# Feature-major input blocks that begin 0, 16 or 32 bytes into tiles 32 bytes longer

## The chip, the cores and the metric

The kernel runs on one NeuronCore of a Trainium2 chip. The metric is the device time of one execution in microseconds (us); lower is better.

## The reference

The program is the forward pass of a two-layer decoder trunk over 256 tokens with a width of 2048, all in float32. Every layer is: normalise, mix, add to the residual; normalise, SwiGLU, add to the residual.

- Layer 0 mixes with one input projection of 12,336 columns, whose parts feed an mLSTM head group and a Mamba-2 SSD head group (with a causal convolution); both outputs go through one output projection.
- Layer 1 mixes with causal attention of 16 heads (with 256 tokens a query has only its own block) between a projection to q, k, v and an output projection.
- The SwiGLU has 5632 hidden columns: `(silu(x @ w_gate) * (x @ w_up)) @ w_down`.
- A last normalisation ends the trunk.

Almost all of the arithmetic is in products of a 256-row activation with a large weight matrix.

## The kernel before, in words

**Two-part numbers.** Every large product is made of float32r matmuls. A weight tile `raw` is split on the chip into a high part `wh` (ScalarE, L365 and L439) and the rest `wl` (VectorE, L366 and L441). An activation is split the same way into a high and a low part, and three products, high by high, high by low and low by high, are summed in PSUM (L472 to L474, L411 to L413; in `lin_w` the first and the third are one matmul of 512 columns at L381, and the second is one of 256 columns at L385).

**Feature-major activations.** A `KT` object holds one activation with the 2048 features along the partitions: four blocks of 128 partitions by 4 feature groups by 2 parts by 256 tokens, that is 8192 bytes in each partition. A block is written by `turned` (transposes on TensorE into PSUM, then L225 to L229 split them into the block), and then it is only read. Where a KT lives is its `home`. The inputs of the big projections, `xa` (layer 0), `x1`, `x2` and `x3` (written by `normed_later`), have the home `long`. The other KT objects (`mx`, half of `my`, `ha`, `hb`, `o`) live in pools of the current stage. The first half of `my` calls `long` too, by a function of its own.

**What `long` is.** It takes one of six tiles of 8192 bytes a partition from the pool `res`, which lies near the start of the on-chip memory (SBUF). Besides the four blocks of a KT, `qT` and `kT`, and later the two residual tiles `xr_` (`xres`), live there. The pool `res` also has four `small` tiles of 4096 bytes behind the six.

**Order in memory.** Pools are laid one behind the other: `pad`, `res`, `cst`, `sml`, `pad2`, `tmp`, and then the pools of the stage: MIXER, and after it staging tiles for the weights with JOIN, FFN and ATTN in turn. `pad`, `pad2` and the `gap` entries are tiles that nothing reads or writes. As the pools are laid out before, every block of a KT, every weight tile and every `tmp` tile begins at a multiple of 256 bytes.

**Who reads the blocks.** In `lin_w` (q, k, the convolved columns; in layer 1 q and k) the block is the moving operand, streamed through TensorE, and the weights are loaded as the stationary operand. In `lin_a` (v and o) and in `block` (the z columns, both SwiGLUs' gate and up, v of layer 1) a 128-token piece of the block is loaded as the stationary operand, and the weights are streamed. `block` replaces some pairs of feature groups (plan letter S) by seven products with sums of weights and of activations (`acc_e`, `sums`, `skx`, `skh`).

**Order of the work.** TensorE is fed in program order. Weights come by DMA through the SyncE queue into a ring of tiles; the splits have a raised priority; small pieces of the mixers are put between matmuls by a list of due times (`later`, `tick`). A tile of a later stage that lies on memory of an earlier one waits for that one's last user.

The lines that allocate a block and a `long` tile:

```python
    def long(shape, name, dt=F32):
        return res.tile(shape, dt, tag="res", name=name)
...
                self.blocks[b] = self.home([P, 4, 2, T], f"{self.name}{b}", F32R)
```

Of the kernel before, what the change touches and what calls it, by code (L numbers as in the profile page):

```python
# [9 lines left out]
F32 = mybir.dt.float32  # L10
F32R = mybir.dt.float32r
# [6 lines left out]
P = 128  # L18
T = 256
NT = T // P  # L20
D = 2048
# [19 lines left out]
PLAN_H = {4: "PSPSPPPP", 3: "PSPSPP"}  # L41
PLAN_H_LATE = "PPSPSP"
STAGING = tuple({tag: 1} for tag in "raw1 raw2 wh1 wh2 wl1 raw0 wh0 wl0 wl2".split())
MIXER = ({"raw": 4, "wh": 3, "wl": 3}, {"cb": 1}, {"rows": 3}, {"hm": 2}, {"gap": 192}, {"ba": 4}, {"cols": 2}, {"wide": 2})
JOIN = ({"rawx": 1}, {"gap": 256}, {"blk": 2})
FFN = ({"rawx": 1}, {"skh": 2}, {"blk": 4}, {"gf": 4})
ATTN = ({"blk": 4}, {"qk": 4}, {"v": 2}, {"rope": 1, "mask": 1})
# [18 lines left out]
def hybrid_trunk(ctx: ExitStack, tc: tile.TileContext, a: dict, out: bass.AP):  # L66
# [3 lines left out]
    res = ctx.enter_context(tc.tile_pool(name="res", bufs=6))  # L70
    cst = ctx.enter_context(tc.tile_pool(name="cst", bufs=1))
    sml = ctx.enter_context(tc.tile_pool(name="sml", bufs=2))
    pad2 = ctx.enter_context(tc.tile_pool(name="pad2", bufs=1))
    pad2.tile([P, 40], F32, name="pad2")
    tmp = ctx.enter_context(tc.tile_pool(name="tmp", bufs=9))
    psm = ctx.enter_context(tc.tile_pool(name="psm", bufs=1, space=PSUM))
    drp = ctx.enter_context(tc.tile_pool(name="drp", bufs=1, space=DRAM))
# [20 lines left out]
    def open_stage(name, pools):  # L98

        close_stage()
        for guard, pool, tags in open_pool(name, pools):
            stage["guards"].append(guard)
            stage["pools"].append((pool, tags))
        stage["spare"] = any("rawx" in tags for tags in pools)
# [8 lines left out]
    def held_tile(tag, shape, name, dt=F32):  # L116
        for pool, tags in stage["pools"] + staging:
            if tag in tags:
                return pool.tile(shape, dt, tag=tag, name=name, bufs=tags[tag])
        raise KeyError(tag)  # L120
# [21 lines left out]
    def wide(shape, name, dt=F32):  # L142
        return held_tile("wide", shape, name, dt)

    def long(shape, name, dt=F32):
        return res.tile(shape, dt, tag="res", name=name)

    def t2(shape, name, dt=F32):
        return tmp.tile(shape, dt, tag="tmp", name=name)
# [19 lines left out]

    open_stage("m", MIXER)  # L170

# [19 lines left out]
    rows = t2([P, P], "rows")  # L191
# [64 lines left out]
    class KT:  # L256
# [4 lines left out]

        def block(self, b):
            if self.blocks[b] is None:
                self.blocks[b] = self.home([P, 4, 2, T], f"{self.name}{b}", F32R)
            return self.blocks[b]

        def parts(self, k):
# [276 lines left out]

    w_in = a["l0_w_in"]
    xt0 = KT("xa", KD, long)
    ss0 = cst.tile([P, NT, 4], F32, name="ss0")

# [5 lines left out]
    def input_ready(k, last):  # L554
# [15 lines left out]
        elif c < 4 and c > 1 and k == 4 * c - 2:  # L570
            with tc.high_priority(offset=40):
                input_part(c)

    qT = long([P, MH, T], "qT")
    kT = long([P, MH, T], "kT")
    banks_q = lin_w(w_in, C_Q, xt0, KD, ready=input_ready)
    for c in range(4):
# [107 lines left out]
    cols = held_tile("cols", [P, NT, P], "cols")  # L685
# [28 lines left out]
    hm = [held_tile("hm", [P, MH, MDV + 1], f"hm{t}") for t in range(NT)]  # L714
# [85 lines left out]
    cb, y = [], []  # L800
# [92 lines left out]
    def add_blocks(w, kt, row, nk, plans, finish=None, begin=None, whole=None, pairs=None, ahead=((), ())):  # L893

        for q in range(2):
            c0 = 2 * q * STRIP
            dst = [xr_[t][:, c0 + n_ * STRIP:c0 + (n_ + 1) * STRIP] for t in range(NT) for n_ in range(2)]

            def add_all(what):
                for d, x in zip(dst, what):  # L900
                    nc.vector.tensor_add(d, d, x)

            if begin is not None:
                begin(2 * q)
                begin(2 * q + 1)
            final = q and whole is not None
            F, _ = block(((w, c0), (w, c0 + STRIP)), kt, row, nk, plans[q], add_all, 2 if final else 1, pairs and list(pairs),
                         ahead[q])
            if final:
                for t in range(NT):  # L910
                    with tc.high_priority(offset=1600):
                        for i in (2 * t, 2 * t + 1):
                            for n, cut in enumerate(halved if i == 3 else (slice(0, STRIP),)):
                                nc.vector.tensor_add(dst[i][:, cut], dst[i][:, cut], F[i][:, cut])
                                finish(i - 2 * t + 2, t, n, cut)
                        whole(t)
                continue
            with tc.high_priority(offset=1600):
                add_all(F)
            if finish is not None:  # L920
                for s in (2 * q, 2 * q + 1):
                    finish(s)
# [38 lines left out]
    for q in range(2):  # L961
        F, pre = block(tuple((w_in, C_Z + (2 * q + n) * STRIP) for n in range(2)), xt0, 0, KD, PLAN_X if q else PLAN_LATE,
                       ahead=((5, scale_gated, 0),) if q else ((4, sums_of, xt0, 1),))
        if q == 0:
            for s in range(4):
                need(("y", s))
        for i in range(4):
            with tc.high_priority(offset=1600):
                nc.vector.tensor_add(pre[i], pre[i], F[i])
        for t, n, piece in gate_pieces(q):  # L970
            th = t2([P, STRIP], "thz")
            nc.scalar.activation(th, pre[2 * t + n], AF.Tanh, scale=rh0[:, t:t + 1])
            nc.vector.scalar_tensor_tensor(th, th, 1.0, pre[2 * t + n], op0=OP.add, op1=OP.mult)
            nc.vector.scalar_tensor_tensor(piece, th, rh0[:, t:t + 1], piece, op0=OP.mult, op1=OP.mult)
# [17 lines left out]
    def ffn(xt, r, wg_, wu_, wd, name, finish, begin=None, whole=None):  # L992
# [6 lines left out]
        def hidden(hT, i, s, plan):  # L999
            F, pre = block(((wg_, s * STRIP), (wu_, s * STRIP)), xt, 0, KD, plan)  # L1000
            hs = []
            for t in range(NT):
                g, u = F[2 * t], F[2 * t + 1]
                if pre is not None:
                    for p, f in zip(pre[2 * t:2 * t + 2], (g, u)):
                        with tc.high_priority(offset=1600):
                            nc.vector.tensor_add(p, p, f)
                    g, u = pre[2 * t:2 * t + 2]
                h = t2([P, STRIP], "h")
                nc.scalar.activation(h, g, AF.Tanh, scale=rh[:, t:t + 1])  # L1010
                nc.vector.scalar_tensor_tensor(h, h, 1.0, g, op0=OP.add, op1=OP.mult)
                nc.vector.scalar_tensor_tensor(h, u, rr[:, t:t + 1], h, op0=OP.mult, op1=OP.mult)
                hs.append(h)
            transpose_later(hT, i, hs, None, 1, 0)
# [182 lines left out]
```

## Time and profile before

| what | value |
|---|---|
| time, median of two runs | 2580.15 us (2579.81 and 2580.49) |
| the profiled execution: span from the first to the last instruction | 2578.2 us |
| its mean granted TensorE clock | 0.999 |
| TensorE matmuls, busy | 2563.5 us, 99% of the span, 12,222 |
| TensorE weight loads, busy (beside the matmuls) | 2130.7 us, 83% |
| VectorE | 2196.5 us, 85% |
| ScalarE | 1454.3 us, 56% |
| read from HBM | 492.26 MB, 192 GB/s over the span |

The profile shows one execution. "Busy" of TensorE counts a matmul from its start to a modelled end, and consecutive matmuls overlap, so the distance from one start to the next says more than the duration. The profile names instructions by source line, engine, operation, written and read tile; PE is TensorE, PEld its weight loads, DVE VectorE, ACT ScalarE, POOL GpSimd, SP SyncE. The launch adds to the span what lies before the first instruction and after the last: 2580.15 - 2578.2 = 1.95 us against the median.

### The profile page before, as it was taken

What the parts mean: (1) busy time and instruction counts of PE and PEld (TensorE: products, weight loads), DVE (VectorE), ACT (ScalarE), POOL (GpSimd) and SP (SyncE); (2) the same over time, 40 slices, a digit from 0 to 9 for tenths busy, and PEclk for the clock granted to TensorE, in tenths of its full rate; (3) what the DMA queues carried; (4) which work ended last, traced back from release to release, by engine and by line L of the source; (5) the groups of instructions that cost most, each with busy time, mean ns of one, the idle gap of its engine ahead of it and who ended that gap; (6) DMA issues with size and microseconds to landing.
All of it is one profiled execution on the core that took longest, in us unless ns stands there. A gap on an engine that the chain in (4) does not pass through costs nothing.

```text
span 2578.2 us, 32660 instructions
## 1 busy us (share of the span) xinstructions
PE 2563.5 (99%) x12222; PEld 2130.7 (83%) x12222; DVE 2196.5 (85%) x2831; ACT 1454.3 (56%) x1929; POOL 43.6 (2%) x77
## 2 busy tenths in 40 slices
PE   9999999999999999999999999999999999999998
PEld 8888888888888888888888888888888888888887
DVE  6676777799989998899889986767999888988898
ACT  6465665566665554555455665666655545554554
POOL 2000010000000000000000000000000000000000
PEclk9999999999999999999999999999999999999999
DMA  7566576566564656465656556554555655565554
GB/s 237 170 211 182 166 235 182 163 205 212 185 213 163 215 194 212 163 226 188 206 167 225 186 174 229 164 180 146 180 192 200 212 181 199 193 213 191 199 188 154
DMA packets 254767, 496.55 MB, mean 193 GB/s; under 512 B 15704, under 2 KB 16608, under 8 KB 254352
## 3 DMA queue, kind: packets, MB, share of 16 engines
q1 hardware_dynamic: 250384, 483.26, 57.1%
q0 software_dynamic: 2896, 8.51, 1.1%
q10 hardware_dynamic: 1328, 2.70, 0.3%
q8 instruction: 96, 1.57, 0.2%
q14 instruction: 63, 0.52, 0.1%
HBM read 492.26 MB, written 2.14 MB: 192 GB/s over the span
## 4 chain that ended last, share of the span: by engine, by line
PE 90%; DVE 5%; issue 2%; DMA 2%; ACT 1%; SPq 0%; POOL 0%; POOLq 0%; DVEq 0%; ACTq 0%
PE acc_f L473 18%; PE acc_f L474 18%; PE acc_f L472 17%; PE acc_w L381 11%; PE acc_w L385 5%; PE acc_e L472 4%; PE acc_e L473 4%; PE acc_e L474 4%; PE acc_a L412 2%; PE acc_a L413 2%; PE acc_a L411 2%; DVE wl L441 2%; PE p_tr L282 2%; PE p_y L866 1%; DMA raw<-in_l_w_o 1%
## 5 line engine op out<-in xcount | busy, mean ns | idle before, releaser
L439 ACT CAST wh<-raw 128x1024 fp32r<-128x1024 f32 (+1 forms) x577 | 630.0, 1134 | 412.9 <-PE acc_f L474 338.1
L441 DVE TENSOR_TENSOR wl<-raw,wh 128x1024 fp32r<-128x1024 f32 (+1 forms) x577 | 748.7, 1323 | 79.1 <-ACT wh L439 73.8
L474 PE MATMUL acc_f<-wh,x 128*128 128x512 f32 x1122 | 438.2, 391 | 0.0
L473 PE MATMUL acc_f<-wl,x 128*128 128x512 f32 x1122 | 437.5, 390 | 0.1
L472 PE MATMUL acc_f<-wh,x 128*128 128x512 f32 x1122 | 436.5, 391 | 0.0
L366 DVE TENSOR_TENSOR wl<-raw,wh 128x1024 fp32r<-128x1024 f32 (+1 forms) x225 | 271.3, 1218 | 139.8 <-ACT wh L365 137.3
L439 ACT CAST wh<-sums 128x1024 fp32r<-128x1024 f32 x222 | 227.9, 1051 | 225.9 <-PE acc_f L474 137.7
L365 ACT CAST wh<-raw 128x1024 fp32r<-128x1024 f32 (+1 forms) x225 | 231.9, 1044 | 196.3 <-PE acc_w L381 111.6
L441 DVE TENSOR_TENSOR wl<-sums,wh 128x1024 fp32r<-128x1024 f32 x222 | 266.7, 1221 | 34.6 <-ACT wh L439 34.1
L473 PEld LDWEIGHTS acc_f<-wl,x 128*128 128x128 f32 x1122 | 210.7, 188 | 44.9 <-DVE wl L441 1.9
L474 PEld LDWEIGHTS acc_f<-wh,x 128*128 128x128 f32 x1122 | 210.7, 188 | 43.1
L472 PEld LDWEIGHTS acc_f<-wh,x 128*128 128x128 f32 x1122 | 210.6, 188 | 42.6
L381 PE MATMUL acc_w<-xa,wh 128*128 128x512 f32 x768 | 207.5, 398 | 1.5 <-DVE xa L229 1.5
L381 PEld LDWEIGHTS acc_w<-xa,wh 128*128 128x128 f32 x768 | 138.8, 189 | 27.9 <-DVE xa L229 1.6
L448 DVE TENSOR_TENSOR sums<-raw 128x1024 f32<-128x1024 f32 x111 | 135.4, 1220 | 12.9 <-DMA raw<-in_l_ffn_up 8.0
L381 PE MATMUL acc_w<-x,wh 128*128 128x512 f32 x512 | 138.9, 399 | 0.0
L385 PE MATMUL acc_w<-xa,wl 128*128 128x256 f32 x768 | 121.8, 282 | 0.0
L385 PEld LDWEIGHTS acc_w<-xa,wl 128*128 128x128 f32 x768 | 110.1, 190 | 6.7
L474 PE MATMUL acc_f<-wh,hb 128*128 128x512 f32 (+1 forms) x284 | 109.6, 387 | 0.0
L473 PE MATMUL acc_f<-wl,hb 128*128 128x512 f32 (+1 forms) x284 | 109.6, 387 | 0.0
L472 PE MATMUL acc_f<-wh,hb 128*128 128x512 f32 (+1 forms) x284 | 109.5, 387 | 0.0
L472 PE MATMUL acc_f<-wh,ha 128*128 128x512 f32 x280 | 109.0, 390 | 0.0
(362 smaller groups left out, 4581.3 us busy)
## 6 DMA issues: line engine op xcount, KB each, us to landing
raw<-in_l_w_in SPq DMA_DIRECT2D x191, 512.0 KB, 3.7
raw<-in_l_ffn_gate SPq DMA_DIRECT2D x176, 512.0 KB, 3.9
raw<-in_l_ffn_up SPq DMA_DIRECT2D x176, 512.0 KB, 4.8
raw<-in_l_ffn_down SPq DMA_DIRECT2D x176, 512.0 KB, 5.2
raw<-in_l_w_qkv SPq DMA_DIRECT2D x96, 512.0 KB, 4.7
raw<-in_l_w_out SPq DMA_DIRECT2D x64, 512.0 KB, 5.2
raw<-in_l_w_o SPq DMA_DIRECT2D x32, 512.0 KB, 4.9
rows<-scr POOLq DMA_DIRECT2D x10, 512.0 KB, 5.2
```

Of the source, the lines that this page charges most:

```text
L282: nc.tensor.transpose(pt[:, j * T + t * P:j * T + (t + 1) * P], src[t][:, c:c + P], ident)
L365: nc.scalar.copy(wh[:, ks, :], raw[:, ks, :])
L366: nc.vector.tensor_sub(wl[:, ks, :], raw[:, ks, :], wh[:, ks, :].bitcast(F32))
L381: return nc.tensor.matmul(banks[f], wh[:, kk, f * P:(f + 1) * P], kt.both(k0 + kk), start=k0 + kk == 0, stop=False, skip_group_check=True)
L385: nc.tensor.matmul(banks[f][:, :T], wl[:, kk, f * P:(f + 1) * P], kt.parts(k0 + kk)[0], start=False, stop=k0 + kk == nk - 1, skip_group_ch ...
L411: nc.tensor.matmul(banks[t], xh[:, ts], wh[:, kk, :], start=k0 + kk == 0, stop=False)
L439: nc.scalar.copy(h[:, c, :], of[:, c, :])
L441: nc.vector.tensor_sub(l[:, c, :], of[:, c, :], h[:, c, :].bitcast(F32))
L448: nc.vector.tensor_sub(sums[:, 0:2, :], raw[:, 2:4, :], raw[:, 3:0:-2, :])
L472: nc.tensor.matmul(dst, ah, bh, start=start, stop=False)
L473: nc.tensor.matmul(dst, ah, bl, start=False, stop=False)
L474: nc.tensor.matmul(dst, al, bh, start=False, stop=stop)
```

## The change

`long` gets a parameter `line`. Each `long` tile becomes 2056 float32 (8224 bytes) long, and what is used of it begins `4 * line` floats, that is 16 times `line` bytes, into it. Block `b` of a KT whose home is `long` is given `line = b % 3`, so blocks 0, 1, 2, 3 begin 0, 16, 32 and 0 bytes into their tiles. `qT`, `kT`, `xres` and the two blocks of `my` keep 0. The unused tile `pad2` grows by 64 bytes, and the gap of 192 bytes in MIXER goes. No instruction is added, removed or given another shape.

```diff
-MIXER = ({"raw": 4, "wh": 3, "wl": 3}, {"cb": 1}, {"rows": 3}, {"hm": 2}, {"gap": 192}, {"ba": 4}, {"cols": 2}, {"wide": 2})
+MIXER = ({"raw": 4, "wh": 3, "wl": 3}, {"cb": 1}, {"rows": 3}, {"hm": 2}, {"ba": 4}, {"cols": 2}, {"wide": 2})
...
-    pad2.tile([P, 40], F32, name="pad2")
+    pad2.tile([P, 56], F32, name="pad2")
...
-    def long(shape, name, dt=F32):
-        return res.tile(shape, dt, tag="res", name=name)
+    def long(shape, name, dt=F32, line=0):
+        whole = res.tile([P, D + 8], dt, tag="res", name=name)[:, 4 * line:4 * line + D]
+        if len(shape) == 2:
+            return whole
+        names = "abcd"[:len(shape) - 1]
+        return whole.rearrange(f"p ({' '.join(names)}) -> p {' '.join(names)}", **dict(zip(names, shape[1:])))
...
-                self.blocks[b] = self.home([P, 4, 2, T], f"{self.name}{b}", F32R)
+                self.blocks[b] = self.home([P, 4, 2, T], f"{self.name}{b}", F32R, *([b % 3] if self.home is long else []))
```

## The prediction

> **What bounds the kernel now.** I read the page's busy table first, then its chain, then the waits, and then the groups and the timeline for TensorE alone.
>
> ```profile
> PE 2563.5 (99%) x12222; PEld 2130.7 (83%) x12222; DVE 2196.5 (85%) x2831; ACT 1454.3 (56%) x1929; POOL 43.6 (2%) x77
> ...
> PEclk9999999999999999999999999999999999999999
> ...
> PE 90%; DVE 5%; issue 2%; DMA 2%; ACT 1%; SPq 0%; POOL 0%; POOLq 0%; DVEq 0%; ACTq 0%
> ```
>
> TensorE is busy 99% of the span at its full clock, and 90% of the chain that ended last is its matmuls. The waits say who gives way to whom:
>
> ```profile
> ACT wh L439 <- PE acc_f L474: 475.8, 213, 5.5
> ```
>
> ```profile
> PE acc_w L381 <- DVE xa L229: 1.5, 2, 0.8
> ...
> PE p_tr L282 <- DMA xin<-in_x: 0.2, 1, 0.2
> ```
>
> The splitting of weights waits 475.8 us for matmuls to free its tiles; the longest wait of the matmuls, in the second list, is 1.5 us in all. So VectorE, ScalarE and the DMAs run ahead of TensorE and have room. A change is worth what it does to the distance between the starts of two matmuls, times their number.
>
> That distance stands in the timeline. First a stretch where x1 is the stationary operand (27 matmuls of 512 columns, the first and the last shown), then one where xa is streamed.
>
> ```profile
> 899.66 0.39 PE L474 MATMUL acc_f<-wh,x 128*128 128x512 f32 x1
> ...
> 905.55 0.39 PE L473 MATMUL acc_f<-wl,x 128*128 128x512 f32 x1
> ```
>
> ```profile
> 222.17 2.00 PE L381 MATMUL acc_w<-xa,wh 128*128 128x512 f32 x8
> 224.01 1.11 PE L385 MATMUL acc_w<-xa,wl 128*128 128x256 f32 x8
> 224.96 0.40 PE L381 MATMUL acc_w<-xa,wh 128*128 128x512 f32 x1
> ```
>
> The first gives (905.55 - 899.66) / 26 = 0.2265 us for a matmul, the second (224.01 - 222.17) / 8 = 0.230 us for 512 columns and (224.96 - 224.01) / 8 = 0.119 us for 256. Durations are longer than distances, because neighbours overlap.
>
> **The change part by part.** No instruction comes or goes, none changes its shape, its engine or its queue, and no wait is added. Only start addresses move, so the price is the difference in duration of instructions that read or write at the new places. These are the readers on TensorE:
>
> ```profile
> L474 PE MATMUL acc_f<-wh,x 128*128 128x512 f32 x1122 | 438.2, 391 | 0.0
> ...
> L381 PE MATMUL acc_w<-xa,wh 128*128 128x512 f32 x768 | 207.5, 398 | 1.5 <-DVE xa L229 1.5
> ...
> L381 PE MATMUL acc_w<-x,wh 128*128 128x512 f32 x512 | 138.9, 399 | 0.0
> ...
> L385 PE MATMUL acc_w<-xa,wl 128*128 128x256 f32 x768 | 121.8, 282 | 0.0
> ...
> L472 PE MATMUL acc_f<-wh,ha 128*128 128x512 f32 x280 | 109.0, 390 | 0.0
> ...
> L411 PE MATMUL acc_a<-wh,xa 128*128 128x512 f32 x256 | 100.7, 393 | 0.0
> ...
> L472 PE MATMUL acc_f<-wh,xa 128*128 128x512 f32 x98 | 38.2, 391 | 0.0
> ...
> L472 PE MATMUL acc_e<-wh,x 128*128 128x512 f32 x69 | 26.8, 389 | 0.0
> ```
>
> Streamed: 768 + 512 matmuls at L381 and as many at L385, 2,560. Stationary: three products each of 1122, 98 and 69 in `block` and of 256 in `lin_a`, 4,635. Together 7,195 of 12,222 (the gate's 48 and a few sums left out). Three of the four blocks move inside their tile, and since the tiles now step by 8,224 bytes, a tile that was j-th in the pool also begins 32 times j bytes later. By the order of allocation xa has tiles 0, 5, 4, 3 and x1 to x3 have 4, 3, 0, 5, so the blocks end up 0, 48, 32 and 32 bytes past a multiple of 64 in both. A quarter of the readers, those of block 0, keep their alignment to 64.
>
> Does a start that is off cost TensorE anything? The kernel before has one streamed operand with shifted starts: `v`, whose heads are 264 floats apart (`slot_a([P, MH, MDV + 8], ...)`), so that the eight heads begin 0, 32, 64 to 224 bytes past a multiple of 256. And it has one stationary operand, the gate weights `wgh`, with rows of 96 floats, 0 or 128 past.
>
> ```profile
> L744 PEld LDWEIGHTS p_num<-v,dec x48: 188/190/193, 162.4 to 350.9; 128*128 128x128 f32 x48
> L744 PE MATMUL p_num<-v,dec x48: 377/380/382, 162.5 to 351.1; 128*128 128x257 f32 x48
> ```
>
> ```profile
> L637 PEld LDWEIGHTS p_gate<-xa,wgh x16: 161/162/165, 101.9 to 107.2; 128*96 128x96 f32 x16
> L637 PE MATMUL p_gate<-xa,wgh x16: 278/281/283, 102.0 to 107.3; 128*96 128x256 f32 x16
> ```
>
> ```profile
> L1102 PE MATMUL p_o<-pT,v 128*128 128x256 f32 x32 | 9.5, 379 | 0.0
> ```
>
> Columns are minimum/median/maximum in ns. All 48 matmuls on `v` lie within 5 ns, and with one column more they are 1 ns longer than those of L1102, whose operands are aligned. So steps of 32 bytes cost nothing there. Two limits of this row: `v` is plain float32, which the trace shows as two matmuls for each one in the program, and no operand of TensorE begins 16 bytes past a multiple of 32, as block 1 will. I take 0 ns for each reader, since L744 is the nearest row, and keep both ends below.
>
> The writers, VectorE and ScalarE, have shifted rows of their own:
>
> ```profile
> L792 DVE SCALAR_TENSOR_TENSOR cv<-xr,convw,cv 128x255 f32<-128x255 f32 x32 | 15.4, 482 | 0.6
> ...
> L792 DVE SCALAR_TENSOR_TENSOR cv<-xr,convw,cv 128x253 f32<-128x253 f32 x32 | 15.2, 476 | 0.0
> ...
> L229 DVE SCALAR_TENSOR_TENSOR xa<-p_tr,pv,xa 128x256 fp32r<-128x256 f32 x16 | 7.4, 480 | 1.4 <-ACT xa L228 1.2
> ...
> L764 ACT ACTIVATE hm<-hm,rrm 128x256 f32<-128x256 f32 x16 | 7.3, 502 | 0.1
> ...
> L959 ACT ACTIVATE y<-y,rrg 128x256 f32<-128x256 f32 x16 | 6.8, 498 | 2.7 <-POOL rrg L221 2.7
> ```
>
> L792 writes 4 to 12 bytes past an aligned start and takes what the aligned L229 takes for the same number of elements; `hm` has rows of 1,028 bytes and its scaling costs 4 ns more than that of the aligned `y`. Some hundred such instructions at 4 ns would be 0.4 us on engines that wait for TensorE: nothing.
>
> The pads. The six longer tiles push what lies behind them by 192 bytes, `pad2` makes it 256 for `tmp` and all stage pools, and the missing gap leaves 64 for `ba`, `cols` and `wide` in MIXER. Weight tiles and staging keep their alignment. What lands at a new offset by DMA is `xin` (64 bytes off) and `xres` (32 and 64).
>
> ```profile
> xin<-in_x SPq DMA_DIRECT2D x4, 128.0 KB, 3.8
> ...
> out<-xres SPq DMA_DIRECT2D x4, 256.0 KB, 2.5
> ```
>
> Only the first load and the last store are exposed. If a shift made the transfers an eighth longer, 0.5 us at the start and 0.3 us at the end; I take 0 and keep 0.8 us as the end. [...]
>
> The sum: 2578.2 us of span plus 1.95 us around it plus 0 is 2580 us, the median.
>
> **The rivals.**
>
> A clash that goes (faster). The weight load of the next matmul runs beside the streaming of this one, and with all blocks and weight tiles at multiples of 256 bytes the two reads might meet in the same lines. For it: a float32r matmul of 512 columns takes 389 to 391 ns, and L1102 with 256 columns in two passes, so as many column steps, 379; at most 10 ns for each reader could be such a clash. Against it: 390 is also what `ha` shows, in another pool, and the distance of 0.2265 us doesn't vary with the block or the weight tile, though these lie at many distances; and the two streams advance at different rates (0.45 ns a column against 0.9, worked out below), so that another start would shift the meetings and not end them. Price: three quarters of 7,195, 5,396, times 10 ns is 54 us, so 2526; for half of it 2553. It passes 2% (52 us) only where the whole 10 ns go.
>
> [...]
>
> A read that runs into one more unit (slower). If SBUF is read in units of 64 bytes, or 16 columns, then 2 KB from an unaligned start take 33 units and not 32. The slope is in the groups: (398 - 282) / 256 = 0.45 ns a column, so 16 columns are 7 ns. Place: the streamed operand in `lin_w`, 2,560 times three quarters times 7 ns = 13 us, so 2593. The stationary operand pays too, but beside a matmul: at L744 and L637 it takes 190 ns for 128 columns and 162 for 96, 0.9 ns a column, so 16 columns more are 14 ns, and 226 - 190 = 36 are to spare. Only if they were exposed would 4,635 times three quarters times 14 ns = 49 us come on top: 2642, slower by over 2%. It decides from 52 us / 5,396 = 9.6 ns for each shifted reader. Against it: the 5 ns spread of L744 over eight starts, half of which are off 64.
>
> That the change doesn't do what it says: the step of the tiles adds to the step of the blocks, and blocks 2 and 3 both land at 32. Then whatever the places were meant for happens for fewer blocks; the time is the forecast's.
>
> **How the numbers follow.** No effect, 2577 to 2584: 0.68 (with the last rival in it). One more unit in streaming, 2593: 0.12. Half a clash gone, 2553: 0.09. The whole clash gone, 2526: 0.06. Unit and load exposed, 2642: 0.05. The likeliest is 2580. It and the unit hold 0.80 only just, so the range also reaches to half a clash: 2553 to 2600, which leaves out 0.11. Faster by over 2%: 0.06; slower by over 2%: 0.05; within 2%, about what a measurement of this kernel can tell from no change: 0.89.
>
> **What would show it.** If I am right, the groups of L472 to L474 on x stay at 389 to 391 ns, L381 at 398 and L385 at 282, and the 1,333 matmuls of this window, inside the first SwiGLU, stay that many within a few:
>
> ```profile
> 1000.00:1300.00 300.00, 300.00 (x1333) 245.55 (x1332) 264.95 (x288) 154.27 (x159) 0.00 (x0) 1.00 0.59 198
> ```
>
> The first count is that of the matmuls in 300 us, and the 1.00 is the granted clock. A unit shows at L381 and L385 alone, by 7 ns, on blocks 1 to 3; a clash as a distance below 0.2265 us in `block`, while `ha` and `hb` keep theirs. Loads of 202 ns at blocks 1 to 3 with longer distances are the exposed load. I would be wrong if the distance depends on the low bits of both addresses together, which no row of an aligned kernel can show.

## The result and the profile after

The changed kernel takes 2606.2 us (median of two runs, 2606.08 and 2606.32) against 2580.15 before: a ratio of 1.0103, 95% interval 1.0074 to 1.0132. It is 26 us slower. The forecast was 2580, and its range ended at 2600.

The page of the changed kernel: the span, the busy table, the granted clock and the chain by engine.

```profile
span 2604.6 us, 32660 instructions
...
PE 2592.6 (100%) x12222; PEld 2133.6 (82%) x12222; DVE 2200.2 (84%) x2831; ACT 1454.2 (56%) x1929; POOL 43.5 (2%) x77
...
PEclk9999999999999999999999999999999999999999
...
PE 96%; issue 1%; DVE 1%; DMA 1%; ACT 0%; POOL 0%; SPq 0%; POOLq 0%; ACTq 0%; DVEq 0%
```

The same instructions run at the same granted clock, 0.999 in both kernels. TensorE's busy time grew by 29.1 us, the span by 26.4 us, and the matmuls' share of the chain from 90% to 96%. So the matmuls themselves became longer; no new wait did it. All line numbers from L146 on are now 4 higher. These are the groups of the changed kernel, named as in the prediction (count, busy us, mean ns of one, idle before).

```profile
L478 PE MATMUL acc_f<-wh,x 128*128 128x512 f32 x1122 | 444.4, 396 | 0.0
L476 PE MATMUL acc_f<-wh,x 128*128 128x512 f32 x1122 | 443.9, 398 | 0.0
L477 PE MATMUL acc_f<-wl,x 128*128 128x512 f32 x1122 | 442.6, 395 | 0.0
...
L385 PE MATMUL acc_w<-xa,wh 128*128 128x512 f32 x768 | 209.6, 401 | 0.5 <-DVE xa L233 0.3
L389 PE MATMUL acc_w<-xa,wl 128*128 128x256 f32 x768 | 121.6, 282 | 0.0
L478 PE MATMUL acc_f<-wh,ha 128*128 128x512 f32 x280 | 109.2, 391 | 0.0
L415 PE MATMUL acc_a<-wh,xa 128*128 128x512 f32 x256 | 101.8, 398 | 0.0
L478 PE MATMUL acc_f<-wh,mx 128*128 128x512 f32 x104 | 41.2, 396 | 0.0
```

The weight load of the first product, in the kernel before (L472) and in the changed one (L476):

```profile
L472 PEld LDWEIGHTS acc_f<-wh,x 128*128 128x128 f32 x1122 | 210.6, 188 | 42.6
```

```profile
L476 PEld LDWEIGHTS acc_f<-wh,x 128*128 128x128 f32 x1122 | 210.8, 188 | 48.0
```

These rows show which operand pays. Where the block on `long` is stationary, in the first three rows, one matmul takes 395 to 398 ns instead of 390 to 391; L415 went from 393 to 398. Where it is streamed, 512 columns take 401 instead of 398 and 256 columns 282 as before. `ha`, which did not move, stays at 391. `mx` lies behind the removed gap and pays too. The weight load is 188 ns in both kernels.

The timeline of the same kind of stretch as before (x1 stationary, 27 matmuls, first and last shown; start, duration):

```profile
905.22 0.40 PE L478 MATMUL acc_f<-wh,x 128*128 128x512 f32 x1
...
911.29 0.39 PE L477 MATMUL acc_f<-wl,x 128*128 128x512 f32 x1
```

(911.29 - 905.22) / 26 = 0.2335 us from start to start, where it was 0.2265. In the window inside the first SwiGLU, 1318 matmuls begin in 300 us where 1333 did:

```profile
1000.00:1300.00 300.00, 300.00 (x1318) 243.11 (x1317) 263.73 (x288) 153.57 (x157) 0.00 (x0) 1.00 0.58 199
```

To find where the 26.4 us are, I added up the distances from each matmul's start to the next one's over the whole timeline, by what they read, and subtracted the sums of before. The sums include what few waits there are.

```
stationary: x1 +8.5, x3 +8.4, x2 +1.8, xa (block) +1.3, xa (lin_a) +2.6,
            skx +2.3, mx +1.4, my +0.5, o -1.0, ha, hb and skh together +0.3
streamed:   lin_w 512 columns +2.4, lin_w 256 columns -1.5
the rest:   -0.5
```

Ordered by where the stationary operand begins, modulo 256 bytes, with the streamed weights at 0 throughout, the mean distance of the 512-column matmuls (those below 260 ns, to keep waits out) is this. In the kernel before, all begin at 0, and the mean is 227.3 ns.

```
bytes    0      32     64     96     112    128    160    176    192
ns       227.6  233.0  233.2  234.2  232.9  232.4  233.4  230.3  230.9
```

### The profile page after: what moved, and what is told of

It reads as the page before. It is cut to its first block, busy times and chain, and to the rows that moved or that the text cites. A ratio compares the mean times of both kernels' runs of the same rounds, so it can differ in the third digit from the quotient of the medians.

```text
span 2604.6 us, 32660 instructions
## 1 busy us (share of the span) xinstructions
PE 2592.6 (100%) x12222; PEld 2133.6 (82%) x12222; DVE 2200.2 (84%) x2831; ACT 1454.2 (56%) x1929; POOL 43.5 (2%) x77
## 4 chain that ended last, share of the span: by engine, by line
PE 96%; issue 1%; DVE 1%; DMA 1%; ACT 0%; POOL 0%; SPq 0%; POOLq 0%; ACTq 0%; DVEq 0%
PE acc_f L476 19%; PE acc_f L478 19%; PE acc_f L477 19%; PE acc_w L385 11%; PE acc_w L389 5%; PE acc_e L476 4%; PE acc_e L477 4%; PE acc_e L478 4%; PE acc_a L416 2%; PE acc_a L415 2%; PE acc_a L417 2%; PE p_tr L286 2%; PE p_y L870 1%; PE p_num L748 0%; DVE wl L445 0%
## 5 line engine op out<-in xcount | busy, mean ns | idle before, releaser
L443 ACT CAST wh<-raw 128x1024 fp32r<-128x1024 f32 (+1 forms) x577 | 630.1, 1133 | 431.9 <-PE acc_f L478 357.3
L445 DVE TENSOR_TENSOR wl<-raw,wh 128x1024 fp32r<-128x1024 f32 (+1 forms) x577 | 749.3, 1324 | 90.9 <-ACT wh L443 85.5
L478 PE MATMUL acc_f<-wh,x 128*128 128x512 f32 x1122 | 444.4, 396 | 0.0
L476 PE MATMUL acc_f<-wh,x 128*128 128x512 f32 x1122 | 443.9, 398 | 0.0
L477 PE MATMUL acc_f<-wl,x 128*128 128x512 f32 x1122 | 442.6, 395 | 0.0
L443 ACT CAST wh<-sums 128x1024 fp32r<-128x1024 f32 x222 | 227.5, 1049 | 233.0 <-PE acc_f L478 144.7
L445 DVE TENSOR_TENSOR wl<-sums,wh 128x1024 fp32r<-128x1024 f32 x222 | 266.9, 1222 | 36.6 <-ACT wh L443 36.2
L477 PEld LDWEIGHTS acc_f<-wl,x 128*128 128x128 f32 x1122 | 210.9, 188 | 50.6 <-DVE wl L445 1.1
L476 PEld LDWEIGHTS acc_f<-wh,x 128*128 128x128 f32 x1122 | 210.8, 188 | 48.0
L477 PE MATMUL acc_f<-wl,hb 128*128 128x512 f32 (+1 forms) x284 | 109.8, 388 | 0.0
L476 PE MATMUL acc_f<-wh,hb 128*128 128x512 f32 (+1 forms) x284 | 109.7, 387 | 0.0
```

Source lines behind the costliest of these rows:

```text
L443: nc.scalar.copy(h[:, c, :], of[:, c, :])
L445: nc.vector.tensor_sub(l[:, c, :], of[:, c, :], h[:, c, :].bitcast(F32))
L476: nc.tensor.matmul(dst, ah, bh, start=start, stop=False)
L477: nc.tensor.matmul(dst, ah, bl, start=False, stop=False)
L478: nc.tensor.matmul(dst, al, bh, start=False, stop=stop)
```

## The experiments

In the expectations, theory A says that a float32r matmul is slower where its two operands begin at different places modulo 256 bytes. Each difference below is against the kernel before unless it says otherwise.

**Only the step of the tiles and the pads.** The changed kernel with all blocks at 0 in their tiles:

```diff
-..., *([b % 3] if self.home is long else []))
+..., *([0] if self.home is long else []))
```

> The changed kernel with all four blocks at byte 0 of their longer tiles; the tiles still step by 8,224 bytes, and ba, cols and wide stay 64 bytes off. Theory A: what costs is that the start of the stationary operand is no longer a whole multiple of 256 bytes away from that of the streamed weights, by whatever amount. Blocks of xa then stand at 0, 160, 128, 96 past a multiple of 256, those of x1 to x3 at 128, 96, 0, 160, as many off as in the changed kernel: 2602 to 2608 us. Theory C: the 16 bytes of block 1 and the 32 of block 2 themselves cost: back to 2580 to 2588 us.

It took 2604.57 us, ratio 1.0088 (1.0071 to 1.0105). Its groups:

```profile
L477 PE MATMUL acc_f<-wl,x 128*128 128x512 f32 x1122 | 443.9, 396 | 0.0
L478 PE MATMUL acc_f<-wh,x 128*128 128x512 f32 x1122 | 442.3, 394 | 0.0
L476 PE MATMUL acc_f<-wh,x 128*128 128x512 f32 x1122 | 441.4, 396 | 0.0
```

So nearly all of the loss is there without the starts that the change is named after: tiles 8,224 bytes apart put the j-th 32j bytes further on.

**Blocks 64 bytes on, the rest in place.** No longer tile, no new view; two pads trade 64 bytes:

```diff
-    pad.tile([P, 32], F32, name="pad")
+    pad.tile([P, 48], F32, name="pad")
-    pad2.tile([P, 40], F32, name="pad2")
+    pad2.tile([P, 24], F32, name="pad2")
```

> The kernel before with the pool res (all feature-major inputs, qT, kT, xres, the activation sums skx, and the small constants) 64 bytes further on, and every other pool where it was (pad 16 floats longer, pad2 16 shorter). All tiles keep a step of 8,192 bytes. Theory A: some 5,700 stationary loads off by 64 bytes at 5 to 6 ns each: 2608 to 2618 us, and the groups of acc_f on x at 396 to 398 ns. Theory B: a unit of 64 bytes (or 32) is what counts, as the prediction had it: 2580 us, groups at 390 to 391.

**Everything 64 bytes on.** The first of these two edits alone, so that weights and blocks move together:

> The kernel before with everything 64 bytes further on (pad 16 floats longer, nothing else), so that no operand of a large matmul starts at a multiple of 256 bytes, but all stand at the same remainder of 64. If only the distance between the two operands counts (theory A): 2579 to 2582 us. If each start must itself be a multiple of 256 (theory D): all large matmuls pay, 8,700 times 5 to 6 ns and more, 2625 to 2640 us.

The first took 2606.04 us, ratio 1.0095 (1.008 to 1.011), the second 2582.47, ratio 1.0005 (0.9995 to 1.0014). One group of each, first with the blocks moved alone, then with all moved:

```profile
L474 PE MATMUL acc_f<-wh,x 128*128 128x512 f32 x1122 | 444.7, 396 | 0.0
```

```profile
L474 PE MATMUL acc_f<-wh,x 128*128 128x512 f32 x1122 | 438.2, 391 | 0.0
```

This pair is the main evidence. The blocks begin at the same 64 in both; the matmuls are long in one and short in the other. So it is not the block's own alignment that costs, but its distance from the weights. That rules out the read of one more unit. The prediction's unit of 64 bytes would have been paid in neither kernel, since a start 64 bytes on is a whole unit further; a unit of 128 or 256 bytes would have been paid in both.

**Only the gap.** The entry `{"gap": 192}` taken out of MIXER and nothing else, so that `ba`, which holds `mx`, begins 64 bytes past the weights:

> The kernel before without the gap of 192 bytes in MIXER, the one part of the change that doesn't touch the feature-major inputs: ba, cols and wide begin 64 bytes past a multiple of 256. Theory A: the stationary loads on mx, 324 of them, are off by 64 bytes: acc_f on mx from 390 to 396 to 398 ns, the whole 2 us longer, 2582. Theory C: no change, 390 ns and 2580.

One run gave 2583.38 us, beside 2581.38 for the kernel before.

```profile
L474 PE MATMUL acc_f<-wh,x 128*128 128x512 f32 x1122 | 438.1, 391 | 0.0
...
L474 PE MATMUL acc_f<-wh,mx 128*128 128x512 f32 x104 | 41.2, 397 | 0.0
```

In the kernel before:

```profile
L474 PE MATMUL acc_f<-wh,mx 128*128 128x512 f32 x104 | 40.6, 390 | 0.0
```

`mx` pays 6 to 7 ns (390 with all moved together), `x` nothing: the effect follows the distance into another pool. The 1.4 us of `mx` in the changed kernel come from this edit.

**A map of distances.** The 22 blocks of `ha` and `hb`, both stationary and in no `long` tile, are given 21 starts (0 twice), and the weights stay at 0; other tiles keep their places modulo 256:

```diff
+        off = places["h"].pop(0)
+        whole = held_tile("blk", [P, D + 64], "at_" + words[off], dt)[:, off // 4:off // 4 + D]
```

> The kernel before with the 22 blocks of the two hidden activations (ha, hb) at 22 starts in tiles 256 bytes longer: 0, 16, 32 ... 240 bytes past a multiple of 256 (tiles named by 16-byte lines), and 4, 8, 24, 248 and 252. All weights stay at multiples of 256. Theory A (only a whole multiple of 256 bytes between the two operands is free): the groups of zero lines at 389 to 391 ns, every other, the single bytes too, at 393 to 398; about 20 blocks of 72 matmuls at 4 to 6 ns each, 2587 to 2589 us. Theory E (what counts is the 16-byte line, seen from its number): 4 and 8 bytes in as zero, 24 bytes as one line, 248 and 252 as fifteen lines; nearly the same time.

One run: 2588.34 us beside 2580.54. The tiles are named by their start in 16-byte lines; the rows give minimum/median/maximum ns, from the view of a single tile, for starts of 0, 16, 32, 64 and 4 bytes.

```profile
L479 PE MATMUL acc_f<-wh,at_zero_lines x40: 389/389/397, 950.1 to 2094.9; 128*128 128x512 f32 x40
```

```profile
L479 PE MATMUL acc_f<-wh,at_one_lines x20: 389/389/393, 958.9 to 1013.8; 128*128 128x512 f32 x20
```

```profile
L479 PEld LDWEIGHTS acc_f<-wh,at_two_lines x32: 187/188/192, 967.1 to 1024.7; 128*128 128x128 f32 x32
L479 PE MATMUL acc_f<-wh,at_two_lines x32: 392/395/400, 967.3 to 1025.0; 128*128 128x512 f32 x32
```

```profile
L479 PE MATMUL acc_f<-wh,at_four_lines x20: 393/398/398, 1207.0 to 1261.1; 128*128 128x512 f32 x20
```

```profile
L479 PE MATMUL acc_f<-wh,at_four_bytes x20: 388/393/478, 2521.3 to 2565.7; 128*128 128x512 f32 x20
```

The mean distance from start to start, by bytes past 256:

```
0: 227.0   4: 232.1   8: 230.6  16: 227.4  24: 230.5  32: 233.0  48: 233.3
64: 233.2  80: 231.9  96: 233.8 112: 233.2 128: 232.9 144: 233.0 160: 233.4
176: 229.7 192: 229.6 208: 232.7 224: 233.1 240: 229.2 248: 233.4 252: 229.9
```

Theory A holds with one exception: 16 bytes are nearly free in this map, though two kernels below show that they are not always. Theory E does not fit: 4 and 8 bytes cost something, and 24 bytes more than 16. There is no slope with the distance. 4, 8 and 24 bytes cost 3.5 to 5 ns, 32 to 160, 208, 224 and 248 about 5 to 7, and 176, 192, 240 and 252 between 2 and 3. At 252 the mean mixes two paces: the first 33 of its 66 matmuls start 226 to 227 ns apart, most of the others 233 to 234. The load takes 188 ns at 32 bytes as well.

**Only the low halves.** The low part of each `ha` and `hb` block begins 64 bytes off, the high part at 0; in `block` the order is high by `wh` (L475), high by `wl` (L476), low by `wh` (L477).

```diff
+        whole = held_tile("blk", [P, D + 64], name, dt)[:, :D + 32]
+        return whole.rearrange("p (b x) -> p b x", b=2)[:, :, :D // 2].rearrange("p b (a t) -> p a b t", a=4)
```

> The kernel before with the low halves of the hidden activations (ha, hb), and they alone, 64 bytes past a multiple of 256; the high halves and all weights stay. In the program the products come as high by wh, high by wl, low by wh (lines 475, 476, 477 of this file). Theory F: what is slowed is the matmul whose streaming runs beside the load of the off operand, that is the one before it: high by wl (476) from 390 to 394 to 398 ns, the others 390. Theory G: a matmul pays when its own two operands are off: low by wh (477) grows, the others don't. Either way some 560 matmuls at 6 ns: 2583 to 2584 us.

One run: 2586.28 us beside 2580.54, some 2 us more than expected.

```profile
L477 PE MATMUL acc_f<-wh,ha 128*128 128x512 f32 x280 | 111.1, 398 | 0.0
L476 PE MATMUL acc_f<-wl,ha 128*128 128x512 f32 x280 | 109.6, 392 | 0.0
...
L475 PE MATMUL acc_f<-wh,ha 128*128 128x512 f32 x280 | 109.0, 391 | 0.0
```

The low half is loaded while L476 streams: in the kernel before, the load for the third product (L474) starts at 2560.49 us and the matmul of the second (L473) at 2560.48. L476 takes 392 ns; L477, whose own operand lies off, takes 398. From start to start it is 228.7, 229.3 and 235.2 ns after L475, L476 and L477, where the kernel before has 226.9 to 227.4. So the matmul that uses the displaced operand pays most, and not the one that streams while it is loaded. By the recorded starts, this speaks against a collision of the load with the stream beside it, which is how the prediction had imagined its clash; it does not exclude one, since the trace doesn't show when the operands are read.

**Only the starts in the tiles.** Blocks at 0, 16, 32 and 0 as in the changed kernel, but tiles 256 bytes longer, and the pads and the gap of before; for room, the reserve for dynamic DMA descriptors is 6,144 instead of 8,192 bytes here and in the four kernels below:

```diff
-        return res.tile(shape, dt, tag="res", name=name)
+        whole = res.tile([P, D + 64], dt, tag="res", name=name)[:, 4 * line:4 * line + D]
```

> The starts of the change (0, 16, 32, 0 bytes into the tile) without its other parts: the long tiles are 256 bytes longer and not 32, so each begins at a multiple of 256, and the gap of 192 bytes and pad2 are as before. The room comes from the scratch for software DMA descriptors, 6144 bytes and not 8192. By the map (start 0 and start 16 at a median of 389 ns, start 32 at 395): only block 2 pays, some 1,050 stationary loads at 5.7 ns, 6 us: 2585 to 2588 us. If the starts within the tiles are what costs in the changed kernel and the longer step isn't: 2598 to 2606 us. If start 16 was free in the map only by its neighbours: block 1 pays as well, 2591 to 2594.

It took 2588.43 us, ratio 1.0028 (1.0018 to 1.0038). Block 2, 32 bytes off, has a mean distance of 232.9 ns; block 1 (of x1 to x3), 16 off, 229.1 with a median of 227; blocks 0 and 3 keep 227. So the named starts alone cost 8 us, and the step with the pads 23; the changed kernel's 26 are less than both together, because what counts is the distance that results: block 2 of x1 to x3, which lies in tile 0, is at 0 by the step alone and at 32 with the start, while block 1 goes only from 96 to 112.

**All blocks 16 bytes on**, in the same tiles, to see whether the start that is nearly free is of use:

```diff
+..., *([1] if self.home is long else []))
```

> As the run before, but all four blocks begin 16 bytes into their tiles (and so past a multiple of 256), qT, kT and xres at 0. If a distance of 16 bytes is as free as 0: 2579 to 2583 us, block's groups at 389 to 391 ns; up to 3 us less if the streamed operand of the 256-column products gains as it did at 64 bytes (119 to 117 ns). If 16 is free only by its neighbours in the map: 4,635 loads at 5 ns, 2602 to 2606 us.

It took 2584.03 us, ratio 1.0011 (1.0003 to 1.002).

```profile
L478 PE MATMUL acc_f<-wh,x 128*128 128x512 f32 x1122 | 439.2, 392 | 0.0
...
L389 PE MATMUL acc_w<-xa,wl 128*128 128x256 f32 x768 | 120.0, 279 | 0.0
```

By the sums of distances, the streamed 256-column matmuls gain 3.0 us, and `lin_a` (+2.2), the 512-column ones (+1.5), x1 and x3 (+2.1 together) give back more.

The time fits neither case of the expectation, and the timeline shows why: at 16 bytes there are two paces. The lines below show the same block of xa in the first call of `lin_a`, which was interrupted by a wait for a weight split, and in the second, which was not. Of each stretch two matmuls are shown, 18 distances apart.

```profile
139.01 0.50 PE L416 MATMUL acc_a<-wl,xa 128*128 128x512 f32 x1 [0.93 <-DVE wl L370]
...
139.57 0.39 PE L415 MATMUL acc_a<-wh,xa 128*128 128x512 f32 x1
...
143.78 0.39 PE L415 MATMUL acc_a<-wh,xa 128*128 128x512 f32 x1
```

```profile
188.00 0.39 PE L415 MATMUL acc_a<-wh,xa 128*128 128x512 f32 x1
...
192.08 0.39 PE L415 MATMUL acc_a<-wh,xa 128*128 128x512 f32 x1
```

(143.78 - 139.57) / 18 = 0.2339 us, and (192.08 - 188.00) / 18 = 0.2267. I sorted all stretches of at least 18 such matmuls without a break of 260 ns or a matmul of another kind, by their mean from the eleventh on. Of 88 at 16 bytes, 57 run at 226.6 to 227.2 ns and 31 at 232.6 to 233.5, and none between. In the kernel before, all 79 run at 226.6 to 228.3; with the blocks 64 bytes on, all 63 at 232.9 to 234.7. The kernel with only the starts in the tiles has both paces in block 1 too, 8 stretches at the one and 9 at the other, and its time lies between the first and the third case of its expectation. So 16 bytes are free or cost 6 ns, and the distance alone doesn't decide which. Right before 22 of the 31 slow stretches, and 4 of the 57 fast ones, lies a distance of 260 ns or more, so the pace often changes at an interruption. What sets it was not tried.

**Only `lin_w`'s weights off.** Since the 256-column matmuls were quicker with all blocks 16 bytes on (279 ns against 282), `lin_w`'s weight tiles begin 192 bytes on, and `block` and `lin_a` keep theirs at 0 in longer tiles:

```diff
-        for k0, wh, wl in chunks(w, col, nk, KC if ready is None else 1):
+        for k0, wh, wl in chunks(w, col, nk, KC if ready is None else 1, 48):
```

> The kernel before with the weight tiles that lin_w loads (and only those) 192 bytes past a multiple of 256, by a view into tiles 256 bytes longer; everything else, lin_a and block too, at multiples of 256; software DMA scratch 6144 bytes and not 8192. So lin_w has the distance between streamed and stationary operand that it had with res 64 bytes further on, where its 256-column matmuls fell from 282 to 280 ns in duration, and block keeps distance 0. Theory A, with lin_w's gain a property of the distance: 256-column groups at 279 to 280 ns, 512-column at 398, 1,280 times 2 to 3 ns, 2577 to 2579 us, the one version that could beat both. Theory H: lin_w's gain came with the other shifts of that run (constants, transposes): no change, 2580 to 2582.

It took 2586.32 us, ratio 1.002 (1.0011 to 1.0029).

```profile
L389 PE MATMUL acc_w<-xa,wl 128*128 128x256 f32 x768 | 120.0, 279 | 0.0
...
L476 PE MATMUL acc_f<-wh,xa 128*128 128x512 f32 x98 | 39.3, 404 | 2.6 <-ACT wh L443 2.5
```

The 3.0 us came where they were looked for, and the matmuls of the mixers and the z columns (xa in `block`) lost 4.6 and 2.4 us, a new wait of 2.5 us for a weight split among them. Most of the 4.6 us lie at two transposes at 515 and 517 us, where the next start comes 1.1 and 2.8 us later, since TensorE waits there for `tho` and for that split. The longer weight tiles move the mixers' tiles; which of that made the loss was not tried.

**Two controls**, since the last three kernels changed more than an address. The kernel before with the smaller reserve only:

> The kernel before with nothing changed but the reserve for descriptors of dynamic DMAs, 6144 bytes instead of 8192, as the three runs with long tiles 256 bytes longer had it. Theory A (only the distance of the two starts counts): 2580 to 2581.5, ratio below 1.001. Rival: the reserve itself costs 1.5 to 3 us, and then the surplus of the runs with all blocks at 16 (2584.0) and with lin_w's own weight tiles (2586.3) is not the address's: 2582 to 2584.

And the long tiles of 8,448 bytes with all blocks at 0 (and the smaller reserve):

> The kernel before with long tiles 256 bytes longer, all blocks at 0, and the reserve of 6144 bytes: the tiles step by 8448, so that every block and every weight tile again starts at a multiple of 256. Theory A: 2580 to 2582, acc_f on x at 390 to 391 ns. Rival: tiles that are longer than what they hold, or places further on in memory, cost by themselves: 2583 or more, without longer matmuls on x.

They took 2580.53 us, ratio 0.9997 (0.9988 to 1.0006), and 2580.32, ratio 0.9995 (0.9986 to 1.0003). The latter's row:

```profile
L478 PE MATMUL acc_f<-wh,x 128*128 128x512 f32 x1122 | 438.2, 391 | 0.0
```

At this step, a multiple of 256 bytes, the longer tiles cost nothing (391 ns), and neither does the reserve. The surpluses of the three kernels before are therefore theirs. None of the kernels beats the one before.

## Why the prediction was wrong

**What bounds the kernel** was read rightly: TensorE, with every other engine and the DMAs ahead of it. That is why a few ns in each matmul came through to the end nearly undiminished: TensorE's idle time only fell from 14.7 to 12.0 us (span less busy time). The changed kernel's waits of TensorE stay below 1.1 us each.

**The step that failed** is "I take 0 ns for each reader, since L744 is the nearest row". For the 4,635 stationary readers counted there, the measured sum is 8.5 + 8.4 + 1.8 + 1.3 + 2.6 = 22.6 us, or 4.9 ns each. For the 2,560 streamed ones it is 2.4 - 1.5 = 0.9 us, or 0.4 ns each; here 0 was close. L744 (L748 now) is as insensitive in the changed kernel as the prediction said:

```profile
L748 PE MATMUL p_num<-v,dec x48: 378/380/382, 164.4 to 354.1; 128*128 128x257 f32 x48
```

But it is a plain float32 matmul, which the trace shows as two for each one in the program (48 for 24), and its shifted operand is the streamed one. The prediction named the first as a limit of the row and still gave the row the whole forecast; a bound from both sides would have had to leave room for float32r stationary readers at a few ns each. At the 5 ns by which the rows of L744 themselves spread, 4,635 readers would have given 23 us.

**Two classes of readers were missed.** The prediction's paragraph on the pads worked out that `ba` moves by 64 bytes and what lies behind the six tiles by 192, and then looked only for DMAs there. `skx` and `mx` are stationary operands in those places; they cost 2.3 and 1.4 us.

**The clash that goes** had the right pair, the stationary and the streamed operand, and the wrong sign: it took the shared multiple of 256 for the bad state, and it is the good one (227.3 ns from start to start in the kernel before, 230 to 234 off it in the changed one). The argument against it, that 0.2265 us doesn't vary "though these lie at many distances", was empty: all those distances are multiples of 256 bytes, so the kernel before had only one distance in the sense that counts. The prediction's last sentence says just this, as what would make it wrong, and gave it neither a case nor a chance.

**One more unit** was right in sign only. Its 64 bytes were the author's assumption. It had the streamed operand pay 13 us, which paid 0.9, and its exposed-load case had the loads grow by 14 ns, which stayed at 188. Blocks moved by 64 bytes, a whole unit, cost 25 us, and everything moved by 64 bytes costs nothing; no unit fits both.

**The writers and the DMAs at 0** held: the splits of the weights (L443, L445) take 1133 and 1324 ns against 1134 and 1323, VectorE's writes into x and xa (L233) 482 and 481 ns against 479 and 480, and ScalarE's (L232) 473 and 474 against 473 and 475. The loads of `xin` of 128 KB land after 4.0 us instead of 3.8, the stores of 256 KB from `xres` after 2.5 in both, and no wait of TensorE for `xin` above 0.3 us appears; that a shift might lengthen transfers by an eighth was the author's assumption. The blocks land 0, 48, 32 and 32 bytes past a multiple of 64, as worked out; but 64 was the wrong modulus, and at 256 no block of x1 to x3 is left at 0 (they begin at 128, 112, 32 and 160).

**Left open.** What in the hardware makes the state at 0 is not shown, nor why 16 bytes allow two paces. No grid of 16 bytes sorts the map: 16 and 32 bytes, both on it, have 227.4 and 233.0 ns, and 4 and 8 bytes, off it, 232.1 and 230.6; besides, 31 of the 88 stretches at 16 run at 232.6 to 233.5. In these runs the period is 256 bytes, and 32, 64 or 128 is none: they cost about 6 ns each in the map, and in the kernel with tiles of 8,448 bytes, where x stands at odd multiples of 256 bytes from the weights for 1,486 matmuls, these are as short (227.0 ns) as the rest (227.2). That plain float32 is exempt rests on two rows of the changed kernel: L748 (380 ns in both kernels), and L738, where `qT` and `kT` begin 32 and 64 bytes past a multiple of 256 and a matmul of 256 columns takes 378 ns, against 379 before.

## What to carry to other kernels

For float32r matmuls that follow one another closely, keep stationary tiles and streamed tiles at the same remainder of 256 bytes; here every other distance tried cost stationary readers on the mean 2 to 7 ns of 227 for each matmul (16 bytes nothing in some stretches and 6 ns in others), and the change as a whole 1% of the kernel. So choose tile sizes and pads by what they do to every tile behind them: here the longer tiles and the pads alone cost 23 us, the starts that they were made for 8. And before taking a row as evidence that addresses don't matter, ask whether it has more than one address in the sense that is in question, and whether it is of the same kind of matmul and the same operand.

## What the runs showed of the hardware

Not expected was that a float32r matmul's time depends on its two operands' places against each other, while its load took 188 ns with x in place and moved, and at 32 bytes in the map. Moving all operands by 64 bytes changed nothing (391 ns), moving one of them 5 to 7 ns (396 to 398). At 16 bytes whole stretches of the same matmuls run at 227 or at 233 ns from start to start, and none between, so the place alone does not always fix the time. The streamed side answers differently with size: 512 columns became 1 to 3 ns longer in the changed kernel (400 against 399 on x, 401 against 398 on xa), and 256 columns, with all blocks at 16 or `lin_w`'s weights at 192, 3 ns shorter (279 against 282).
